# RWKV layer: the triangular inverses of a group's two head pairs, one after the other or in step

## The chip, the cores and the metric

The kernel runs on one core of one Trainium2 chip. The time is what the device takes for one launch, in microseconds (us). Before the change three runs gave 1012.96, 1013.06 and 1014.63 us; the median is 1013.06 us.

## The reference

One layer of a hybrid decoder is applied to 512 prompt tokens and 8 x 8 sample tokens: an RWKV-7 branch and a differential-attention branch on the same normalised input, gates that merge them, an output projection, a squared-ReLU MLP and a final norm. The change concerns the RWKV branch, whose state follows a recurrence over tokens:

```python
def step(S, inp):
    r_t, w_t, k_t, v_t, a_t, b_t = inp
    sa = jnp.einsum('bhij,bhj->bhi', S, a_t)
    S = S * w_t[:, :, None, :] + sa[..., None] * b_t[:, :, None, :] + v_t[..., None] * k_t[:, :, None, :]
    return S, jnp.einsum('bhij,bhj->bhi', S, r_t)
```

There are eight heads of 64. The term `sa` makes each step depend on the step before it. The kernel works on chunks of 64 tokens, in which these dependences form a unit triangular system; its inverse is what the change is about.

## The kernel before

**Work and stages.** The 576 tokens are split into nine chunks of 64 (eight of the prompt, one that holds the sample tokens). Heads are taken in four pairs, `hp` 0 to 3, with two heads on the 128 partitions; pairs 0 and 1 form group 0, pairs 2 and 3 group 1. For each pair a generator `rwkv(hp)` is run from one `yield` to the next. Its first stage makes the decays, the keys and the products of keys within a chunk (`pn`, `pw`, `pa`, `pk`, `pbn`, `pA`), the second transposes values and keys and starts the sample state (`pV`, `pK`, `pI`), the third inverts the triangular matrices, and the later ones finish the sample state and the output. `chain(0)` and `chain(1)` then carry the state through the nine chunks of a group, both pairs together (`pch`, `pY`).

**The inverse.** Each chunk's 64 x 64 matrix is cut into 32 x 32 blocks. A block's inverse grows in four levels, `l` 1 to 4. A level is a series in which every step needs the one before: TensorE multiplies 36 (levels 3 and 4: 32) blocks into `pW`, ScalarE copies `pW` to `W`, TensorE multiplies as many into `pZ`, VectorE adds `pZ` to `X` and transposes `X` into `Y`, and the next level starts from `X`. After the four levels `pWc` and `pC` join the two 32-blocks of a chunk, and ScalarE puts the result and `Y` together in `TT`, which the chain multiplies with. A program's product in plain fp32 shows as two MATMUL records and two LDWEIGHTS records in the trace, so that a visit of 36 blocks is 72 of each; a dense product in fp32r is one of each.

**What lies between.** `take(n)` sends `n` dense products (128 x 128 by 288 or 296 columns) of the weight streams that wait in a list: the projections `ps_z` and the gates `ps_g`. `blocks()` calls `take(9)` behind every visit, so that TensorE has nine dense products while ScalarE or VectorE work on the result of the visit. Behind `pWc` and `pC` there is none. Numbers such as `take(221)` and `take(106)` between the stages set how much dense work lies elsewhere.

**What sets the order.** [...] The framework's scheduler places the instructions by priority, in the order of the program where no priority is given, and lets a later instruction go ahead when an earlier one is not ready by its own estimate; `issue_after` ties dense products behind a given product. All inverses write to one accumulation bank, `tbank`; the chain's `pY` has another, `cbank(1)`.

The last lines of the program's RWKV part, with the stages in the order in which they are called, are in the diff below.

Of the kernel before, what the change touches and what calls it, by code (L numbers as in the profile page):

```python
# [41 lines left out]
def tile_hybrid_step(ctx, tc, xT, xsT, ktab, vtab, s0T, ptab, w_in, vecs, w2a2, g2, lamv,  # L42
# [6 lines left out]
    def pool(name, bufs=1, stack=ctx, **kw):  # L49
        return stack.enter_context(tc.tile_pool(name=name, bufs=bufs, **kw))  # L50
# [4 lines left out]
    ring = {"job": 0}  # L55

    def act(out, in_, func=AF.Copy, **kw):
        ring["act"] = AE.activation(out=out, in_=in_, func=func, **kw)  # L58

    def tt(out, a, b, op, eng=None):  # L60
        ins = (eng or VE).tensor_tensor(out=out, in0=a, in1=b, op=op)  # L61
        if eng is None:
            ring["tt"] = ins
# [7 lines left out]
    def mm(out, lhsT, rhs, start=True, stop=True):  # L71
        ring["mm"] = PE.matmul(out=out, lhsT=lhsT, rhs=rhs, start=start, stop=stop)  # L72
        return ring["mm"]
# [17 lines left out]
    MUL, ADD, SUB, MAX = ALU.mult, ALU.add, ALU.subtract, ALU.max  # L91
# [12 lines left out]
    def tbank(name):  # L104
        return psc.tile([P, 512], F32, tag="t", name=name)

    def cbank(i, name):
        return (psy if i else psc).tile([P, 512], F32, tag=f"c{i}", name=name)
# [107 lines left out]
    def take(n):  # L216

        while waiting and n:
            if next(waiting[0], None) is None:
                waiting.pop(0)  # L220
            else:
                n -= 1
# [41 lines left out]
    gs = pool("gs", 2, stack=ph1)  # L264

    with tc.tile_pool(name="xin", bufs=2, reuse_waits="tile") as xin:
# [6 lines left out]
        for k in range(0, KT, 4):  # L273
            for j in range(3):
                with prio(FEED + 1000 + 10 * k + j):
                    name = f"raw_{'qkv'[j]}0_{k}"
# [142 lines left out]
    def shifted(i):  # L419
        z = zw.tile([P, 1 + NX], F32, tag="z", name=f"Z{i}")  # L420
        GE.memset(z[:, 0:1], 0.0)

        def f(ps, t0, n):
            tt(z[:, 1 + t0:1 + t0 + n], ps, R1[:, t0:t0 + n], MUL)
        yield from stream(w_in[i], KT, xh, xl, HALFX, f, f"z{i}")
        tz = zw.tile([P, 1 + NX], F32, tag="tz", name=f"tz{i}", bufs=1)
        act(tz, z, scale=v(V_MU + i))
        p = zp.tile([P, NT], F32, tag=f"P{i}" if i >= 12 else f"Pt{i // 4}", name=f"P{i}", bufs=1 if i >= 12 else 2)
        m1 = mu1[:, i:i + 1]
        stt(p[:, :NPR], z[:, 1:1 + NPR], m1, tz[:, 0:NPR], MUL, ADD)  # L430
        s3 = lambda a, o: a[:, o:o + NS].rearrange("p (b t) -> p b t", b=NB)
        stt(s3(p, NPR)[:, :, 1:], s3(z, 1 + NPR)[:, :, 1:], m1, s3(tz, 1 + NPR)[:, :, :7], MUL, ADD)
        stt(p[:, NPR::8], z[:, 1 + NPR:1 + NT:8], m1, tz[:, 1 + NT:], MUL, ADD)
        Pt[i] = p

    def zs(hp):
        return [shifted(i) for i in (hp, 4 + hp, 8 + hp)]

    def gate(g):

        gg = gs.tile([P, NT], F32, tag="gg", name=f"gg{g}")

        def ev(ps, t0, n):
            tt(gg[:, t0:t0 + n], ps, R1[:, t0:t0 + n], MUL)
            act(gg[:, t0:t0 + n], gg[:, t0:t0 + n], AF.Tanh, scale=0.5)
        yield from stream(w_in[26 + g], KT, xh, xl, HALF, ev, f"g{g}")
        nc.sync.dma_start(out=gt_d[g], in_=gg)
# [20 lines left out]
    def branch_b(d):  # L468

        if not ob:  # L470
            ob.extend(ob_halves())
        gg = rt.tile([P, NT], F32, tag="T", name=f"gb{d}", bufs=6)
        nc.sync.dma_start(out=gg, in_=gt_d[KT + d])

        def ev(ps, t0, n):
            stt(gg[:, t0:t0 + n], gg[:, t0:t0 + n], 1.0, ps, ADD, MUL)
        yield from stream(w_brb[d], HB, ob[0], ob[1], HALF, ev, f"brb_{d}")
        nc.sync.dma_start(out=gt_d[KT + d], in_=gg)
# [236 lines left out]
    def m3(ap_, n):  # L715
        q, w = ap_.shape
        return ap_.rearrange("p (o w) -> p o w", o=1).broadcast_to([q, n, w])
# [17 lines left out]
    def rwkv(hp):  # L735
        e = hp % 2
# [131 lines left out]
        for g in range(4):  # L868
            gs = slice(32 * g, 32 * g + 32)
            act(DT[gs], ABR[gs, :, 0, 32 * (g % 2):32 * (g % 2) + 32])  # L870
        Y = rt.tile([P, NCH, 32], F32, tag="Y", name=f"Y{hp}", bufs=2)
        X = rt.tile([P, NCH, 32], F32, tag="X", name=f"X{hp}", bufs=2)
# [1 line left out]
        tt(Y, Y, m3(c[:, C_I32:C_I32 + 32], NCH), ADD)  # L874
        VE.transpose(out=X, in_=Y)

        def blocks(ps, lhs, rhs, n):
            for ci in range(n):
                for g in range(4):
                    gs = slice(32 * g, 32 * g + 32)  # L880
                    last = mm(ps[gs, ci * 32:ci * 32 + 32], lhs[gs, ci], rhs[gs, ci])
            with tc.issue_after(last.ins):
                take(9)
            return ps[:, :n * 32].rearrange("p (c s) -> p c s", c=n)

        with tc.issue_after(ring["mm"].ins):
            take(1)
        for l in range(1, 5):

            n = NCH if l < 3 else 8  # L890
            DM = rt.tile([P, NCH, 32], F32, tag="DM", name=f"DM{hp}_{l}")
            tt(DM[:, :n], DT[:, :n], m3(c[:, C_LM + 32 * l:C_LM + 32 * l + 32], n), MUL)
            W = rt.tile([P, NCH, 32], F32, tag="W", name=f"W{hp}_{l}")
            act(W[:, :n], blocks(tbank(f"pW{hp}{l}"), DM, X, n))
            tt(X[:, :n], X[:, :n], blocks(tbank(f"pZ{hp}{l}"), Y, W, n), ADD)
            VE.transpose(out=Y[:, :n], in_=X[:, :n])
        TT = rb_.tile([P, NCH, 64], F32, tag="TT", name=f"TT{hp}")
        pW = tbank(f"pWc{hp}")
        W = rt.tile([P, NCH, 32], F32, tag="W", name=f"Wc{hp}")
        quads = [(slice(64 * par, 64 * par + 32), slice(64 * par + 32, 64 * par + 64)) for par in range(2)]  # L900
        for ci in range(8):
# [1 line left out]
                mm(pW[b1, ci * 32:ci * 32 + 32], ABR[b0, ci, 0, 32:64], X[b0, ci])  # L903
        for b0, b1 in quads:
            act(W[b1, :8], pW[b1, :256].rearrange("p (c s) -> p c s", c=8))
        pC = tbank(f"pC{hp}")
        for ci in range(8):
            for b0, b1 in quads:
                mm(pC[b0, ci * 32:ci * 32 + 32], W[b1, ci], Y[b1, ci])
        for b0, b1 in quads:  # L910
            act(TT[b0, :8, 32:64], pC[b0, :256].rearrange("p (c s) -> p c s", c=8))
            act(TT[b0, :, 0:32], Y[b0])
            act(TT[b1, :, 32:64], Y[b1])
            GE.memset(TT[b0, 8:, 32:64], 0.0)
            GE.memset(TT[b1, :, 0:32], 0.0)

        own[e] = ST, KBt, TT, ABR, pc
        yield
# [113 lines left out]


    gens = [rwkv(hp) for hp in range(4)]

    def run(*stages):
        for hp in stages:
            while Pt[8 + hp] is None:
                take(2)
            next(gens[hp], None)  # L1040

    waiting += zs(1) + zs(2) + zs(3) + [gate(g) for g in range(KT, 2 * KT)]
    ga = [gate(g) for g in range(KT)]
    waiting += ga[:5]
    run(0, 0)
    take(221)
    run(0, 1, 1)
    take(106)
    run(1)
    chain(0)  # L1050
    run(2, 0, 1, 2, 3)
    take(291)
    run(2, 0, 1, 3)
    take(38)
    run(3)
    waiting += [x for d in range(KT) for x in [branch_b(d)] + ga[5:][d:d + 1]]
    run(0, 1)
    chain(1)
# [237 lines left out]
    for t0, n in LAST:  # L1296
        span, last = slice(t0, t0 + n), []
# [172 lines left out]
```

## Time and profile before

| | |
|---|---|
| median of three runs | 1013.06 us |
| the profiled execution's own time | 1013.38 us |
| its span, first to last instruction | 1011.6 us |
| TensorE, matmul records (PE) | 977.1 us busy, 10012 records |
| TensorE, weight loads (PEld) | 917.7 us busy, 10012 records |
| VectorE (DVE) / ScalarE (ACT) / GpSimd (POOL) | 694.2 / 496.2 / 101.3 us busy |
| mean granted clock of TensorE | 0.994 |
| the four inverses | at 225 to 247, 281 to 302, 394 to 414 and 425 to 446 us |

A busy TensorE is not a TensorE at its peak: matmuls overlap and their ends are modelled, so that the distance from start to start says what one costs. In the rows of the trace `[0.87 <-issue]` is idle time of that engine just before the row, and what ended it; "issue" stands for a start that no semaphore of the profile explains. Runs of equal instructions are merged into one row with a count, and the time in the second column reaches from the start of the first to the end of the last.

### The profile page before, as it was taken

What the parts mean: (1) busy time and instruction counts of PE and PEld (TensorE: products, weight loads), DVE (VectorE), ACT (ScalarE), POOL (GpSimd) and SP (SyncE); (2) the same over time, 40 slices, a digit from 0 to 9 for tenths busy, and PEclk for the clock granted to TensorE, in tenths of its full rate; (3) what the DMA queues carried; (4) which work ended last, traced back from release to release, by engine and by line L of the source; (5) the groups of instructions that cost most, each with busy time, mean ns of one, the idle gap of its engine ahead of it and who ended that gap; (6) DMA issues with size and microseconds to landing.
All of it is one profiled execution on the core that took longest, in us unless ns stands there. A gap on an engine that the chain in (4) does not pass through costs nothing. (4 is left out here: it accounts for less than half of the span.)

```text
span 1011.6 us, 24409 instructions
## 1 busy us (share of the span) xinstructions
PE 977.1 (97%) x10012; PEld 917.7 (91%) x10012; DVE 694.2 (69%) x1445; ACT 496.2 (49%) x1086; POOL 101.3 (10%) x179
## 2 busy tenths in 40 slices
PE   9999999999999999999989999999999999999996
PEld 8999889898888788878889999999999999999996
DVE  6697565964965788345579888966666666666644
ACT  7575563454453353453244666644444444444732
POOL 2511104001010421000210111000000000000001
PEclk9999999999999999999999999999999999999998
DMA  7312663121111235222367633232222222221402
GB/s 272 132 65 97 208 214 100 52 65 44 53 47 56 68 109 172 79 71 89 114 205 222 197 122 99 75 103 85 94 84 87 92 85 84 85 84 43 132 6 94
DMA packets 50833, 105.75 MB, mean 105 GB/s; under 512 B 6066, under 2 KB 8114, under 8 KB 50594
## 3 DMA queue, kind: packets, MB, share of 16 engines
q1 hardware_dynamic: 47442, 96.95, 29.8%
q0 software_dynamic: 1648, 5.35, 1.4%
q10 hardware_dynamic: 1632, 1.89, 0.5%
q8 instruction: 79, 1.29, 0.5%
q14 instruction: 32, 0.26, 0.1%
HBM read 89.38 MB, written 14.78 MB: 103 GB/s over the span
## 5 line engine op out<-in xcount | busy, mean ns | idle before, releaser
L72 PE MATMUL ps_dn<-q,hi_dn 128*128 128x288 f32 x768 | 154.8, 296 | 0.0
L72 PEld LDWEIGHTS ps_dn<-q,hi_dn 128*128 128x128 f32 x768 | 122.9, 188 | 1.4
L72 PE MATMUL ps_dn<-q,lo_dn 128*128 128x288 f32 x384 | 113.3, 295 | 0.0
L72 PE MATMUL ps_g<-xh,hi_g 128*128 128x288 f32 x256 | 80.3, 314 | 0.0
L72 PE MATMUL ps_g<-xh,lo_g 128*128 128x288 f32 x256 | 79.2, 309 | 0.6 <-issue 0.6
L72 PE MATMUL ps_g<-xl,hi_g 128*128 128x288 f32 x256 | 79.3, 310 | 0.0
L72 PEld LDWEIGHTS ps_dn<-q,lo_dn 128*128 128x128 f32 x384 | 72.2, 188 | 0.0
L72 PE MATMUL ps_z<-xh,hi_z 128*128 128x296 f32 (+1 forms) x224 | 67.7, 302 | 1.2 <-DVE Z L61 0.7
L72 PE MATMUL ps_z<-xl,hi_z 128*128 128x288 f32 (+1 forms) x224 | 68.2, 305 | 0.3 <-issue 0.3
L72 PE MATMUL ps_z<-xh,lo_z 128*128 128x288 f32 (+1 forms) x224 | 68.4, 305 | 0.0
L61 DVE TENSOR_TENSOR ya<-ya,ps_dn 128x288 f32<-128x288 f32 x96 | 43.4, 452 | 29.4 <-PE ps_dn L72 29.4
L58 ACT ACTIVATE hi_dn<-raw_dn 128x512 fp32r<-128x512 f32 x48 | 30.1, 628 | 56.1 <-PE ps_dn L72 56.1
L1206 PE MATMUL ua<-h_b,hi 128*128 128x288 f32 x256 | 53.3, 299 | 0.9 <-ACT p L58 0.9
L1206 PE MATMUL ux<-h_t,hi 128*128 128x288 f32 x256 | 52.3, 296 | 0.0
L72 PEld LDWEIGHTS ps_g<-xh,hi_g 128*128 128x128 f32 x256 | 49.0, 192 | 3.2 <-issue 1.6
L58 ACT ACTIVATE c<-c 128x288 f32<-128x288 f32 x112 | 48.5, 440 | 6.6 <-DVE c L61 4.9
L72 PEld LDWEIGHTS ps_g<-xl,hi_g 128*128 128x128 f32 x256 | 49.0, 191 | 2.5 <-issue 0.8
L72 PEld LDWEIGHTS ps_g<-xh,lo_g 128*128 128x128 f32 x256 | 48.9, 191 | 1.4
L58 ACT ACTIVATE hi<-a 128x1024 fp32r<-128x1024 f32 (+1 forms) x32 | 27.0, 845 | 43.1 <-PE ps_dn L72 34.9
L61 DVE TENSOR_TENSOR lo<-s,hi 128x1024 fp32r<-128x1024 f32 x32 | 39.2, 1224 | 10.5 <-ACT hi L58 10.4
L72 PE MATMUL ps_dn<-q,w 128*128 128x320 f32 (+1 forms) x336 | 46.3, 298 | 0.0
L72 PEld LDWEIGHTS ps_dn<-q,w 128*128 128x128 f32 x336 | 45.3, 190 | 0.1
(399 smaller groups left out, 2813.8 us busy)
## 6 DMA issues: line engine op xcount, KB each, us to landing
a<-in_w_up_dram SPq DMA_DIRECT2D x32, 512.0 KB, 3.3
raw_dn<-in_w_down_dram SPq DMA_DIRECT2D x64, 256.0 KB, 2.8
raw_g<-in_w_in_dram SPq DMA_DIRECT2D x32, 256.0 KB, 3.1
raw_z<-in_w_in_dram SPq DMA_DIRECT2D x28, 256.0 KB, 2.8
gt_d<-gg SPq DMA_DIRECT2D x16, 288.0 KB, 2.3
g<-gt_d SPq DMA_DIRECT2D x16, 288.0 KB, 3.4
kp<-in_ktab_dram SPq DMA_DIRECT2D x16, 256.0 KB, 5.0
vp<-in_vtab_dram SPq DMA_DIRECT2D x16, 256.0 KB, 4.2
```

What stands on the lines that cost most here:

```text
L58: ring["act"] = AE.activation(out=out, in_=in_, func=func, **kw)
L61: ins = (eng or VE).tensor_tensor(out=out, in0=a, in1=b, op=op)
L72: ring["mm"] = PE.matmul(out=out, lhsT=lhsT, rhs=rhs, start=start, stop=stop)
L1206: ring["mm"] = PE.matmul(out=ps[:, :288], lhsT=l[:, k], rhs=hb[blk][:, h, k], start=start and i == 0, stop=i == 11, skip_group_check=skip)
```

## The change

A visit now yields, and a new function `invert` drives two generators in turn: one visit of the first pair, one of the second, then twelve dense products. The second pair of a group writes to the chain's bank `cbank(1)`, which is free then. `take(9)` in `blocks` is gone, and twelve dense products now also stand behind the double visits of `pWc` and of `pC`. The stages of the second pair that come ahead of its inverse are called earlier, and the counts of the dense work between the stages are set anew (221, 106 and 291, 38 become 221, 120 and 320, 38).

```diff
-        def blocks(ps, lhs, rhs, n):
+        def blocks(name, lhs, rhs, n):
+            ps = cbank(1, name) if e else tbank(name)
             for ci in range(n):
                 for g in range(4):
                     gs = slice(32 * g, 32 * g + 32)
-                    last = mm(ps[gs, ci * 32:ci * 32 + 32], lhs[gs, ci], rhs[gs, ci])
-            with tc.issue_after(last.ins):
-                take(9)
+                    mm(ps[gs, ci * 32:ci * 32 + 32], lhs[gs, ci], rhs[gs, ci])
             return ps[:, :n * 32].rearrange("p (c s) -> p c s", c=n)
 
-        with tc.issue_after(ring["mm"].ins):
-            take(1)
         for l in range(1, 5):
...
-            act(W[:, :n], blocks(tbank(f"pW{hp}{l}"), DM, X, n))
-            tt(X[:, :n], X[:, :n], blocks(tbank(f"pZ{hp}{l}"), Y, W, n), ADD)
+            act(W[:, :n], blocks(f"pW{hp}{l}", DM, X, n))
+            yield True
+            tt(X[:, :n], X[:, :n], blocks(f"pZ{hp}{l}", Y, W, n), ADD)
             VE.transpose(out=Y[:, :n], in_=X[:, :n])
+            yield True
...
-        pW = tbank(f"pWc{hp}")
+        pW = cbank(1, f"pWc{hp}") if e else tbank(f"pWc{hp}")
...
+        yield True
-        pC = tbank(f"pC{hp}")
+        pC = cbank(1, f"pC{hp}") if e else tbank(f"pC{hp}")
...
+    def invert(*hps):
+
+        with tc.issue_after(ring["mm"].ins):
+            take(1)
+        more = True
+        while more:
+            for hp in hps:
+                more = next(gens[hp], None)
+            with tc.issue_after(ring["mm"].ins):
+                take(12)
+
...
     run(0, 0)
     take(221)
-    run(0, 1, 1)
-    take(106)
-    run(1)
+    run(1, 1)
+    take(120)
+    invert(0, 1)
     chain(0)
     run(2, 0, 1, 2, 3)
-    take(291)
-    run(2, 0, 1, 3)
+    take(320)
+    run(0, 1, 3)
     take(38)
-    run(3)
+    invert(2, 3)
```

The order on TensorE at level 3 of group 0, before (`pW` and `pZ` are the visits of pair 0 alone, `ps_z` the dense products, of which nine stand between two visits):

```order
L72 MATMUL pZ_3414<-W_2_3365,Y_3259 32x32 x36
L72 MATMUL ps_z_1_3249<-xh,lo_z_0_3241 128x296
...
L72 MATMUL pW_3465<-X_3260,DM_3_3462 32x32 x32
L72 MATMUL ps_z_1_3249<-xh,lo_z_1_3245 128x296
...
L72 MATMUL pZ_3531<-W_3_3464,Y_3259 32x32 x32
```

The same place in the changed program (`pZ_4135` and `pW_4222` are of pair 0, `pZ_4170` and `pW_4259` of pair 1; `ps_g` are the dense products, twelve between two double visits):

```order
L72 MATMUL pZ_4135<-W_3_4051,Y_3643 32x32 x32
L72 MATMUL pZ_4170<-W_3_4088,Y_3694 32x32 x32
L72 MATMUL ps_g_0_4042<-xh,lo_g_1_4039 128x288
...
L72 MATMUL pW_4222<-X_3644,DM_4_4219 32x32 x32
L72 MATMUL pW_4259<-X_3695,DM_4_4256 32x32 x32
L72 MATMUL ps_g_1_4043<-xh,lo_g_0_4035 128x288
...
L72 MATMUL pZ_4305<-W_4_4221,Y_3643 32x32 x32
L72 MATMUL pZ_4340<-W_4_4258,Y_3694 32x32 x32
```

Two visits of different pairs now stand back to back. In group 1 all ten visits are double; in group 0 the first `pW` and `pZ` of the two pairs still stand apart, and the other eight are double. So there are 12 + 10 = 22 stretches of small products where there were 40.

The end of group 0's inverses on ScalarE, before (`TT` with the number 4490 is that of pair 1, which the chain waits for):

```order
L58 ACTIVATE TT_4490<-Y_4086 32x9x32 x2
L58 ACTIVATE Wc_4492<-pWc_4491 32x256 x2
L58 ACTIVATE TT_4490<-Y_4086 32x9x32
L58 ACTIVATE hi_g_0_5218<-raw_g_0_5214 128x512
L58 ACTIVATE gg_4287<-gg_4287 128x288
L58 ACTIVATE TT_4490<-pC_4511 32x8x32 x2
L58 ACTIVATE TT_4490<-Y_4086 32x9x32
```

The same place in the changed program (`TT_4405` is pair 0's, `TT_4426` pair 1's):

```order
L58 ACTIVATE Wc_4407<-pWc_4406 32x256 x2
L58 ACTIVATE Wc_4428<-pWc_4427 32x256 x2
L58 ACTIVATE TT_4405<-pC_4459 32x8x32 x2
L58 ACTIVATE TT_4426<-Y_3694 32x9x32
L58 ACTIVATE TT_4426<-pC_4486 32x8x32
L58 ACTIVATE TT_4426<-Y_3694 32x9x32
L58 ACTIVATE TT_4426<-pC_4486 32x8x32
L58 ACTIVATE TT_4426<-Y_3694 32x9x32 x2
```

All four copies of `Y` into pair 1's `TT` now stand behind the copies out of pair 0's `pC`; before, three of pair 1's four went ahead of its own `pC`.

## The prediction

> **What bounds the kernel now.** I read the page's busy times, then the timeline of the four inverses on TensorE and its weight loads, then who waits for what, then the DMA queues.
>
> ```profile
> span 1011.6 us, 24409 instructions
> PE 977.1 (97%) x10012; PEld 917.7 (91%) x10012; DVE 694.2 (69%) x1445; ACT 496.2 (49%) x1086; POOL 101.3 (10%) x179
> q8 instruction: 79, 1.29, 0.5%
> ```
>
> TensorE sets the time. As the dense products are only shifted, the change can move the end only through what lies between TensorE's instructions: switches between small and dense products, and waits. The third row matters later: 79 packets of 16 KB; TensorE's 2 x 10012 records at 256 per packet make 78.
>
> Two visits of pair 0 and the dense products between them:
>
> ```profile
> 225.54 0.82 PE L72 MATMUL pW<-X,DM 32*32 32x32 f32 x72
> 226.29 0.40 PE L72 MATMUL ps_z<-xh,lo_z 128*128 128x288 f32 x1
> 226.52 0.29 PE L72 MATMUL ps_z<-xh,hi_z 128*128 128x288 f32 x1
> ...
> 227.45 0.29 PE L72 MATMUL ps_z<-xl,hi_z 128*128 128x288 f32 x1
> 227.68 0.82 PE L72 MATMUL pZ<-W,Y 32*32 32x32 f32 x72
> 228.42 0.40 PE L72 MATMUL ps_z<-xh,lo_z 128*128 128x288 f32 x1
> L72 PE MATMUL pW<-X,DM x1088: 185/192/213, 225.5 to 439.9; 32*32 32x32 f32 x182
> ```
>
> From 226.52 to 227.45 seven dense products start: 0.133 us each. The first and the last of the nine hold 0.23 us, 0.10 more each. The 72 small ones start over 0.82 less one duration of 0.19, that is 0.63 us (9 ns each), but the first dense product comes 0.75 us after the first small one: the last small one holds 0.12, or 0.11 more. So an alternation costs 0.10 + 0.10 + 0.11 = 0.31 us. The nine fully cover ScalarE's copy here.
>
> Now the weight loads in pair 2's inverse:
>
> ```profile
> 397.43 0.29 PEld L72 LDWEIGHTS pW<-X,DM 32*32 32x32 f32 x25 [0.87 <-issue]
> ...
> 399.15 0.71 PEld L72 LDWEIGHTS pZ<-W,Y 32*32 32x32 f32 x72 [0.16 <-issue]
> ...
> 401.29 0.20 PEld L72 LDWEIGHTS pW<-X,DM 32*32 32x32 f32 x12 [0.16 <-issue]
> 402.41 0.54 PEld L72 LDWEIGHTS pW<-X,DM 32*32 32x32 f32 x52 [0.91 <-issue]
> ...
> 404.38 0.64 PEld L72 LDWEIGHTS pZ<-W,Y 32*32 32x32 f32 x64 [0.16 <-issue]
> ...
> 406.25 0.19 PEld L72 LDWEIGHTS ps_g<-xh,hi_g 128*128 128x128 f32 x1 [0.75 <-issue]
> ```
>
> TensorE stops in the middle of a visit, twelve products into a `pW` whose operands are all there, and no semaphore explains it. Between the second and the third stop lie 52 + 9 + 64 + 3 = 128 weight loads (nine and three of them dense), with their matmuls 256 instructions; between the first two 25 + 9 + 72 + 9 + 12 = 127. That is one packet of q8 each. I read the stops as TensorE waiting for its next block of 256 instructions. Between two stops one block passes: 4.98 and 3.84 us. The others:
>
> ```profile
> 235.65 0.19 PEld L72 LDWEIGHTS ps_z<-xl,hi_z 128*128 128x128 f32 x1 [0.52 <-issue]
> 293.73 0.20 PEld L72 LDWEIGHTS pZ<-W,Y 32*32 32x32 f32 x13 [0.62 <-issue]
> 410.08 0.22 PEld L72 LDWEIGHTS pZ<-W,Y 32*32 32x32 f32 x16 [0.23 <-issue]
> 430.14 0.39 PEld L72 LDWEIGHTS pW<-X,DM 32*32 32x32 f32 x34 [0.22 <-issue]
> 437.80 0.15 PEld L72 LDWEIGHTS pZ<-W,Y 32*32 32x32 f32 x6 [1.03 <-issue]
> ```
>
> From 406.25 to 410.08 is again a block: 3.83 us. All eight stops together are 5.2 us. Elsewhere a block lasts long:
>
> ```profile
> q8 instruction: 21, 0.34, 0.4%
> ```
>
> This is the DMA view from 600 to 950 us, where only large products run: a block every 16.7 us. There a fetch of under 4 us is never seen. In the inverses 72 + 9 products are 162 instructions in 2.14 us (225.54 to 227.68), so 256 in 3.4 us: just faster than a block is fetched.
>
> **The change part by part.**
>
> *Switches.* 40 stretches of small products become 22: 18 x 0.31 = 5.6 us less.
>
> *Instructions per time.* The small products themselves stay. A double visit of levels 1 and 2 with its twelve dense products holds 2 x (144 + 12) = 312 instructions. Free of waits it takes 0.63 + 0.01 + 0.75 = 1.39 us for the small ones and 227.68 - 226.29 = 1.39 plus 3 x 0.133, or 1.79, for the dense ones: 3.18 us, so 256 instructions in 2.61 us. At levels 3 and 4 the 128 small ones are 16 x 0.009 = 0.14 us shorter (1.25 us), and 280 instructions take 3.04 us, 256 in 2.77. The mean is 2.69 us per block, against the 3.83 us or more that a block took between stops. So nearly every block now ends in a stop.
>
> Eight double visits of a group hold 4 x 312 + 4 x 280 = 2368 instructions, 9.25 blocks. The block that follows the one in use has been loaded in the slow stretch ahead, which takes one off: 8 blocks a group, 16 in all. The last two double visits (2 x (64 + 12) = 152 instructions in some 2.9 us) are slow enough.
>
> The price of a block is the unknown. From below 3.4 us, the pace at which the program before ran between stops: 16 x (3.4 - 2.69) = 11.4 us. From above the mean of the three periods, (4.98 + 3.84 + 3.83) / 3 = 4.22: 24.5 us. The 4.98 came while much else was being loaded, and twelve dense products per 3.75 us need fewer weights than nine per 2.14. I take 3.75, just under the two that agree: 16 x 1.06 = 17.0 us.
>
> [...]
>
> *Stops that go.* The eight of before are in the new count, so 5.2 us come off.
>
> *Waits for data.* A `pZ` visit is followed by VectorE's work for both pairs:
>
> ```profile
> 227.39 0.42 DVE L61 TENSOR_TENSOR DM<-DT,cst_sb 128x256 f32<-128x256 f32 x1
> 228.54 0.46 DVE L61 TENSOR_TENSOR X<-X,pZ 128x288 f32<-128x288 f32 x1 [0.73 <-PE pZ L72]
> 229.03 0.48 DVE L896 STREAM_TRANSPOSE Y<-X 128x288 f32<-128x288 f32 x1
> 290.51 0.75 PE L72 MATMUL pW<-X,DM 32*32 32x32 f32 x64 [0.47 <-DVE X L61]
> ```
>
> A level of two pairs needs 2 x (0.42 + 0.46 + 0.48) = 2.7 us of VectorE, and two rounds last 6.2 us even without stops. The next `pW` of pair 1 needs both `X` and, in this order, pair 0's transpose: 0.46 + 0.48 + 0.46 = 1.4 us, of which the first 0.46 can run under pair 1's small products, against 1.79 us of dense cover. I count no change, with 0.5 us either way for the wait at 290.51. `cbank(1)` adds none: the bank's next write needs the copy of its last contents as data anyway.
>
> *The end of a group.* The chain's second product needs both pairs' `TT`:
>
> ```profile
> 301.19 0.44 ACT L58 ACTIVATE TT<-Y 32x288 f32<-32x288 f32 x1
> 302.64 0.77 ACT L58 ACTIVATE TT<-pC 32x256 f32<-32x256 f32 x2
> 303.16 0.30 PE L72 MATMUL pch<-R,TT 64*64 64x64 f32 x2 [0.21 <-ACT TT L58]
> ```
>
> In the new order ScalarE has four copies of `pC` and four of `Y` behind the first `pC`: 2 x 0.77 + 4 x 0.44 = 3.3 us. TensorE has pair 1's `pC` (about 0.6 us) and twelve dense products (1.8) to cover it, and waits some 0.9 us before `chain(0)`, where it waited 0.21: 0.7 us more. Queued behind it are the first steps of the chain. In group 1 other products stand between, so nothing there.
>
> *The dense counts.* Before, 221 + 106 + 291 + 38 and 4 x 73 in the inverses: 948. Now 221 + 120 + 320 + 38 and 2 x 121: 941. Seven products (0.9 us) run later instead; they cost the same there.
>
> Sum: -5.6 + 17.0 - 5.2 + 0.7 = +6.9 us. The profiled execution took 1013.38 us around its span of 1011.6, 0.3 us above the median of 1013.06. So 1020.2, rounded to **1020 us**.
>
> **The rivals.**
>
> *Fetching does not bind (faster).* If blocks come sooner, since less else is loaded, or if the stops have another cause that does not scale with the pace, the double visits run at 3.1 us each. With the stops as before the sum is -5.6 + 0.7 = -4.9: 1008 us. It decides at the price of a block: the sum is zero where 16 x (p - 2.69) = 5.6 + 5.2 - 0.7, at p = 3.32 us. For it: between 225.54 and 230 us no stop shows. Against it: blocks at 3.83 and 3.84 us right after a stop, where nothing but the fetch could be late. [...]
>
> *Data come too late.* If blocks come in time but VectorE, between dense work of its own as at 290.51, makes TensorE wait 0.47 us at each of the 16 double visits of the four levels, 7.5 us come back: -5.6 - 5.2 + 7.5 + 0.7 = -2.6, 1011 us. Against it are the 2.7 us of work in 6.2.
>
> *The clock.* Busy time and granted clock in three stretches:
>
> ```profile
> 399.50:402.90 3.40, 2.60 (x127) 2.29 (x113) 1.91 (x4) 0.44 (x1) 0.00 (x0) 1.00 0.62 196
> 415.60:419.00 3.40, 2.39 (x42) 1.95 (x41) 0.00 (x0) 2.77 (x10) 0.00 (x0) 1.00 0.14 48
> 419.00:422.40 3.40, 3.40 (x16) 3.40 (x16) 0.46 (x1) 1.57 (x6) 0.00 (x0) 0.51 0.00 0
> ```
>
> After a stretch with TensorE busy for 2.39 of 3.40 us the clock fell to half for 3.4 us; after one with 2.60 it did not. The new rounds, busy for 2.69 of 3.75 us (2.44 of 3.40), lie between. A fall costs half of 3.4, 1.7 us; with four in each group 1020 becomes 1034 us.
>
> **How the numbers follow.** The forecast gets 0.70, the fetch that does not bind 0.15, late data 0.10, the clock 0.05. The likeliest case alone runs from 11.4 to 24.5 us for the blocks, so from +1.3 to +14.4: 1014.5 to 1028. The range reaches down to take in the case of late data and leave out most of the faster one: 1009 to 1027. About 2 us (0.2%) is what a measurement of this kernel can tell from no change. Faster: 0.15 and a third of the late data, 0.18. The same: the rest of the late data and the lowest edge of the forecast, 0.10. Slower: 0.72.
>
> **What would show it.** Right: in the changed kernel's inverses TensorE's weight loads stop for about 1 us every 256 instructions, mostly inside the small products, with "issue" as the releaser; two double visits take near 7.3 us instead of 6.2; q8's packets come every 3.5 to 4 us there; the waits of loads for `pW` and `pZ` on "issue" more than double. Wrong: double rounds of 3.2 us without stops (the first rival), waits on VectorE's `X` (the second), a granted clock under 1.00 in the inverses (the third), or a wait at the start of `chain(0)` well above 1 us, which I sized from the order alone.

## The result, and the profile after

In seven runs of each on one chip the changed kernel takes 1019.85 us (median; 1016.30 to 1021.73) and the kernel before 1013.04 (1009.45 to 1014.63). The ratio is 1.0065, with a 95% interval of 1.0045 to 1.0084: slower by 6.8 us. The prediction was 1020 us. The profiled execution of the changed kernel took 1019.11 us around a span of 1017.3, 5.7 us more than that of the kernel before (1013.38 around 1011.6).

The page of the changed kernel, span and busy times:

```profile
span 1017.3 us, 24397 instructions
PE 973.8 (96%) x10012; PEld 918.5 (90%) x10012; DVE 696.2 (68%) x1445; ACT 496.8 (49%) x1086; POOL 100.6 (10%) x179
```

TensorE has the same 10012 matmuls and is busy for 3.3 us less than before, in a span that is 5.7 us longer. So it stands still for longer. Where it does so is seen in the timeline of its weight loads, the view in which the prediction read the stops. First the double visits of group 0, of which only the rows with a stop are shown, and ahead of them one visit that stands in a single row (the number in brackets is idle time just before the row):

```profile
268.15 1.54 PEld L72 LDWEIGHTS pW<-X,DM 32*32 32x32 f32 x144 [0.17 <-DVE Z L61]
...
272.28 1.18 PEld L72 LDWEIGHTS pZ<-W,Y 32*32 32x32 f32 x117 [0.40 <-issue]
277.47 0.19 PEld L72 LDWEIGHTS ps_g<-xh,hi_g 128*128 128x128 f32 x1 [2.60 <-issue]
280.93 0.17 PEld L72 LDWEIGHTS pW<-X,DM 32*32 32x32 f32 x2 [1.19 <-issue]
288.78 0.32 PEld L72 LDWEIGHTS pW<-X,DM 32*32 32x32 f32 x26 [0.27 <-issue]
292.35 0.43 PEld L72 LDWEIGHTS pZ<-W,Y 32*32 32x32 f32 x39 [0.53 <-issue]
```

Then those of group 1:

```profile
407.46 1.33 PEld L72 LDWEIGHTS pW<-X,DM 32*32 32x32 f32 x144 [0.16 <-issue]
410.62 0.68 PEld L72 LDWEIGHTS pZ<-W,Y 32*32 32x32 f32 x69 [0.16 <-issue]
413.20 0.76 PEld L72 LDWEIGHTS pZ<-W,Y 32*32 32x32 f32 x75 [1.91 <-issue]
421.21 1.23 PEld L72 LDWEIGHTS pZ<-W,Y 32*32 32x32 f32 x128 [0.62 <-issue]
425.04 0.18 PEld L72 LDWEIGHTS pZ<-W,Y 32*32 32x32 f32 x3 [2.61 <-issue]
433.99 0.33 PEld L72 LDWEIGHTS pZ<-W,Y 32*32 32x32 f32 x28 [0.39 <-issue]
437.44 0.44 PEld L72 LDWEIGHTS pW<-X,DM 32*32 32x32 f32 x40 [0.46 <-issue]
441.29 0.54 PEld L72 LDWEIGHTS pZ<-W,Y 32*32 32x32 f32 x52 [0.77 <-issue]
445.40 0.19 PEld L72 LDWEIGHTS ps_g<-xl,hi_g 128*128 128x128 f32 x1 [0.66 <-issue]
```

These rows show twelve stops, with idle times of 0.40 + 2.60 + 1.19 + 0.27 + 0.53 = 5.0 us in group 0 and 7.4 us in group 1, 12.4 us in all; the eight of before made 5.2. They lie within a visit (after 69 of 144 loads, after 126 of 128) or among the dense products, and no semaphore ends them. Where nothing stops, the round is as fast as it should be: 407.46 to 410.62, 3.16 us.

What does end them is a packet on q8, the queue of instructions. The packets' own times are in the traces: the one ahead of the stop that ends at 277.47 ran from 275.13 to 276.08 us, the one ahead of 280.93 from 278.51 to 279.51. All twelve stops end 1.2 to 1.6 us after the end of such a packet, and so do the eight of before (1.3 to 1.5 us). Other waits that the rows put down to "issue" do not: the two 0.81-us waits of `ps_g` behind `pF` (355.88 and 510.88 us) come over 10 us after the last packet.

The three rows of waits on "issue" for the tiles of the inverses, before:

```profile
PEld pZ L72 <- issue: 4.3, 18, 1.0
PEld pW L72 <- issue: 4.2, 15, 0.9
PEld ps_g L72 <- issue: 2.4, 3, 0.8
```

and after (us in total, times, the longest):

```profile
PEld pZ L72 <- issue: 8.7, 14, 2.6
PEld ps_g L72 <- issue: 4.9, 4, 2.6
PEld pW L72 <- issue: 3.1, 9, 1.2
```

They come less often, since there are fewer switches (each has its 0.16 us in these rows), and last longer: 16.7 us in place of 10.9.

**Where the 5.7 us come from.** For each pair of neighbouring matmuls I took the median distance from start to start that such a pair has in the trace of before, and summed it over the order of each program. What a start comes later than that was put down to a stop on "issue" in the inverses, to half clock, to a wait for data of over 0.15 us (from 200 to 560 us), or to the rest. From the first to the last matmul's start, in us:

| | order without waits | stops | half clock | waits for data | rest | sum |
|---|---|---|---|---|---|---|
| before | 961.2 | 6.0 | 3.1 | 11.3 | 22.3 | 1003.9 |
| changed | 956.5 | 13.3 | 6.1 | 13.8 | 19.9 | 1009.6 |
| difference | -4.7 | +7.3 | +3.0 | +2.5 | -2.4 | +5.7 |

The stops are 0.8 to 0.9 us larger here than in the rows of weight loads, since this counts what the matmuls lose. "Rest" holds many small deviations and isn't explained further. The first column is an estimate that hangs on which pairs are held to be alike: told apart by the shapes of the products alone, the order of the change comes out 3.7 us shorter than before in place of 4.7, and the difference moves into the rest.

The clock is not a peculiarity of these two executions. Over its seven runs the changed kernel was granted 0.989 of the full clock on average, the kernel before 0.993 to 0.994 in its 71 runs beside the experiments below. If TensorE is busy throughout, 0.004 of 1015 us is some 4 us (an estimate), so that about half of the 6.8 us that the change costs goes by way of the clock.

### The profile page after: what moved, and what is told of

The parts are those of the page before. It is cut to its first block, busy times and chain, and to the rows that moved or that the text cites. A ratio compares the mean times of both kernels' runs of the same rounds, so it can differ in the third digit from the quotient of the medians.

```text
span 1017.3 us, 24397 instructions
## 1 busy us (share of the span) xinstructions
PE 973.8 (96%) x10012; PEld 918.5 (90%) x10012; DVE 696.2 (68%) x1445; ACT 496.8 (49%) x1086; POOL 100.6 (10%) x179
```

## Experiments on the cause: instructions per time, or something else

The theory: TensorE stops because 256 instructions are used up sooner than the next 256 are there; the doubled visits with twelve dense products are only a denser stream. The rival: the stops come with the inverses as such (their operands, their banks, the doubling), and would stay at any pace. The expectations below reckon with 3.3 to 3.8 us or more for a block; the shortest between two stops in any of these traces is 3.45 us. The later times are all against the kernel before on the same chip, which took 1012.79 us in the first set of runs, 1013.48 in the second and 1012.31 in the third.

**Fewer instructions for the same small products.** The tiles of the four levels in bf16, in both kernels:

```diff
-        Y = rt.tile([P, NCH, 32], F32, tag="Y", name=f"Y{hp}", bufs=2)
+        Y = rt.tile([P, NCH, 32], BF16, tag="Yb", name=f"Y{hp}", bufs=2)
...
-            DM = rt.tile([P, NCH, 32], F32, tag="DM", name=f"DM{hp}_{l}")
+            DM = rt.tile([P, NCH, 32], BF16, tag="DM", name=f"DM{hp}_{l}")
```

and DT, X and W alike, with fp32 results at the last level. The changed kernel:

> The changed kernel with the tiles of the inverse's four levels (DT, DM, X, Y, W) in bf16; only the last level's results are written in fp32. The inverse is then computed with fewer digits than the reference asks for. A small product is one matmul and one weight load instead of two of each, so a double round of 2 x (72 + 12) = 168 instructions takes about 3.18 - 0.63 = 2.55 us, 256 instructions 3.9 us: slower than the 3.3 to 3.8 us that a block took between stops. Theory (the pace of instructions is what cost): the small products lose half of 32 visits x 0.63 us = 10 us, and the 13.1 us of stops go too, so 1020 - 10 - 13 = 997 us, range 992 to 1003; 994 if the three half-clock windows behind the stops go with them. Rival (the stops belong to the doubled visits or to their operands, not to the count of instructions): 1020 - 10 = 1010 us with stops left. Second rival: the rounds become so short that VectorE's X and Y come late; then waits of PEld on DVE X of several us.

The kernel before:

> The kernel before with the same tiles in bf16 (the same loss of digits). Theory: small products -10 us, its eight stops (5.2 to 6 us) gone: 1013 - 10 - 6 = 997 us, range 993 to 1002. Beside the changed kernel with bf16 tiles the sign of the whole change should turn round: with no stops in either, the change keeps only its 4.7 us of saved switches, less about 1 us at the start of chain(0) and up to 2.5 us of longer data waits, so the changed one should be 0 to 5 us faster (bf16 against bf16), where in fp32 it was 6.8 us slower. Rival (stops not from the count of instructions): the changed one stays some 6 us slower in bf16 too.

Measured: the changed kernel 991.38 us (987.99 to 993.53), ratio 0.9776 (0.9750 to 0.9802); the kernel before 999.60 us (999.07 to 1001.15), ratio 0.9854 (0.9825 to 0.9884). One round of the changed one at level 3 and the start of the next:

```profile
405.42 0.56 PEld L73 LDWEIGHTS <-Y 32*32 32x32 bf16 x64 [0.17 <-issue]
407.82 0.55 PEld L73 LDWEIGHTS <-DM 32*32 32x32 bf16 x64 [0.17 <-DVE Y L901]
```

The round lasts 2.40 us and holds 2 x (64 + 12) = 152 instructions, 256 in 4.0 us, and no visit is broken: what is left of idle time ahead of a visit in both groups is the 0.16 to 0.17 us of a switch, at two of them 0.2 us more; the granted clock is 0.99 on average from 215 to 450 us. Same doubling, same banks, same twelve dense products, no stops. So the rival falls as far as doubling and banks go; the operands did change their type here, and for them the burst below decides. And the sign of the change turns round: 8.2 us faster in bf16, where it was 6.8 us slower in fp32. I had expected 0 to 5. Part of the surplus is that the kernel before, whose visits are now 1.7 us apart, waits for data inside its inverses. The weight loads, and the matmuls that start with them:

```profile
391.65 0.31 PEld L73 LDWEIGHTS <-DM 32*32 32x32 bf16 x35 [0.35 <-issue]
396.11 0.26 PEld L73 LDWEIGHTS <-DM 32*32 32x32 bf16 x31 [0.79 <-issue]
...
391.64 0.41 PE L73 MATMUL pW<-X,DM 32*32 32x32 bf16 x36 [0.36 <-DVE X L62]
396.11 0.37 PE L73 MATMUL pW<-X,DM 32*32 32x32 bf16 x32 [0.81 <-DVE X L62]
```

Both stand one load into a `pW` visit. Between them lie 35 + 9 + 36 + 9 + 1 + 1 = 91 loads (one of them of `pV`) in 4.46 us, less than the 128 of a block, so they are not stops of the kind above. The rows of the matmuls name what TensorE waited for: VectorE's `X`. By the same account as in the table (medians here over these two traces) the changed kernel saves 7.4 us of order, 2.4 of waits and 2.0 of half clock.

**A burst far from the inverses.** The kernel before with small products that depend on nothing, among the large products of the MLP:

```diff
+            if i == 0 and ch in (3, 5):
...
+                    for j in range(640):
+                        gq = slice(32 * (j % 4), 32 * (j % 4) + 32)
+                        cq = 32 * (j // 4 % 16)
+                        mm(pbu[gq, cq:cq + 32], onesP[gq, :32], onesP[gq, :32])
```

> The kernel before, with two bursts added in the MLP, far from the inverses: 640 fp32 products of 32x32 each on a constant tile, with no operand to wait for, no wait on another engine and a result that nothing reads; 2560 instructions, ten blocks of 256 each. At the second burst, eight extra loads of 256 KB that nothing reads go through another queue. Theory (a block can't be had faster than every 3.3 to 4.2 us): each burst lasts nine or ten times that, 30 to 40 us, with a stop every 256 instructions, and the kernel 1013 + 60 to 80 = 1073 to 1093 us; the second burst, with the extra loads, is the longer one. Rival (instructions are fetched ahead and cost nothing; stops in the inverses have another cause): 1280 matmul records x 9 ns = 11.5 us for each burst, 1013 + 23 = 1036 us.

Measured: 1113.38 us, ratio 1.097 (1.093 to 1.101), 100 us more, where theory said 60 to 80 and the rival 23. The weight loads of the first burst:

```profile
763.64 2.54 PEld L72 LDWEIGHTS pbu<-onesP 32*32 32x32 f32 x184 [0.25 <-issue]
768.18 1.17 PEld L72 LDWEIGHTS pbu<-onesP 32*32 32x32 f32 x128 [1.99 <-issue]
771.92 1.80 PEld L72 LDWEIGHTS pbu<-onesP 32*32 32x32 f32 x128 [2.57 <-issue]
...
797.86 0.41 PEld L72 LDWEIGHTS pbu<-onesP 32*32 32x32 f32 x24 [2.22 <-issue]
```

Exactly 128 loads, with their matmuls 256 instructions, and then a stop, again and again. From 768.18 to 797.86 pass eight blocks: 3.71 us each, at full clock (1.00 in the stretch of the first 128 loads, which take 1.17 us) as at half (0.50 from 770.2 us on, 1.80). All nine stops end 1.3 to 1.5 us after a packet on q8. The operands are constant and the result is read by nobody, so only the instructions can be late. This is the price that the prediction set at 3.75. The fetch is not hidden here: 256 instructions go out in 1.2 to 1.8 us, the first stop comes after 184 loads in a row, and the next ones after each 256 instructions.

The part that I had missed is a lesson on switches. The scheduler set the first 24 small products of the burst one by one between dense ones:

```profile
746.65 0.24 PE L72 MATMUL pbu<-onesP 32*32 32x32 f32 x2
746.83 0.40 PE L72 MATMUL ps_dn<-q,hi_dn 128*128 128x288 f32 x1
747.15 0.24 PE L72 MATMUL pbu<-onesP 32*32 32x32 f32 x2
```

One small and one dense product take 0.50 us; without the switch they would take 0.133 + 2 x 0.009 = 0.15, so an alternation costs 0.35 us (the prediction had 0.31). From 749.8 us on it cost more, at half clock (0.50; 0.78 us a pair), so that 24 pairs filled the 17.0 us from 746.65 to 763.64, 13 us more than their work. With the nine blocks of the burst, 33 us, that is most of its 50. The extra loads of the second burst settle nothing, since they had landed before it: its blocks between two stops last 3.47 to 4.02 us, as in the first (3.47 to 4.01).

**Fourteen dense products in the kernel before**, still one visit after another, to slow the stream without doubling anything:

```diff
             with tc.issue_after(last.ins):
-                take(9)
+                take(14)
...
-    take(221)
+    take(181)
...
-    take(106)
+    take(66)
...
-    take(291)
+    take(213)
```

> The kernel before with fourteen dense products behind each single visit in place of nine; the dense counts between the stages are cut by as many (181, 66, 213, 36), so that 948 dense products lie ahead of the second chain as before. Nothing is in step. A visit with its fourteen products is 172 instructions in about 2.8 us, 256 in 4.2 us. Theory (TensorE's instructions come in blocks of 256, each taking 3.3 us or more): no stop with 'issue' as releaser is left in the inverses, where the kernel before had eight of 5.2 us idle together; the clock falls less; about 1006 us (1004 to 1009). Rival (the stops come with the number of small products, or with the bank or the data they wait for, not with the pace of instructions): the same products and the same number of stops, 1011 to 1014 us.

Measured: 1018.45 us (1016.03 to 1018.96), ratio 1.0047 (1.0027 to 1.0067). The stops went, as said: 0.2 us are left of 6.0. But the kernel became slower, not faster. Three rows of its waits, of weight loads in the stages between the inverses; before, that of `pbn` was 1.3 us and the two of `pA` did not occur:

```profile
PEld pbn L72 <- DVE rkp L66: 2.5, 2, 1.2
PEld pA L72 <- POOL TT L915: 2.3, 1, 2.3
PEld pA L72 <- DVE KB L61: 1.6, 1, 1.6
```

The waits for data rose from 11.3 to 22.2 us. The 160 dense products that went into the inverses (40, 40, 78 and 2 fewer between the stages) were the cover of the stages between them. That is where the gain that I expected went: dense products are the scarce thing here, and an inverse pays for slack with a stage's.

**Six dense products behind each single visit, in step.** The order of the pairs as in the change, but no doubling:

```diff
             for hp in hps:
                 more = next(gens[hp], None)
-            with tc.issue_after(ring["mm"].ins):
-                take(12)
+                with tc.issue_after(ring["mm"].ins):
+                    take(6)
```

> The changed kernel, in step, but with six dense products behind each single visit in place of twelve behind two: the same dense work, no double visit, as many switches as before. A visit with its six is 156 instructions in about 1.75 us, 256 in 2.85 us. Theory: nearly as many stops as in the change and none of the gain from fewer switches, so 1018 to 1024 us, at or above the changed kernel. Rival (it is the double visit as such that costs, by its length or by the work that it puts on VectorE and ScalarE at once): with single visits as before, the time is back at 1011 to 1014 us.

Measured: 1017.29 us (1015.41 to 1018.95), ratio 1.0045 (1.0032 to 1.0058). Slower than before without a single double visit, so the rival falls; the time is just under the 1018 to 1024 of the theory, and a little below that of the change. Some of its stops in group 0:

```profile
275.23 0.54 PEld L72 LDWEIGHTS pW<-X,DM 32*32 32x32 f32 x52 [1.15 <-issue]
278.96 0.64 PEld L72 LDWEIGHTS pZ<-W,Y 32*32 32x32 f32 x64 [0.64 <-issue]
282.53 0.14 PEld L72 LDWEIGHTS pZ<-W,Y 32*32 32x32 f32 x6 [1.31 <-issue]
```

They stand 3.73 and 3.57 us apart, a block each. It has 9.7 us of stops by the account, between the 6.0 of nine dense products a visit and the 13.3 of twelve for two. The order without waits is 961.4 us, as before: no switch is saved, and none was expected to be.

## Experiments on the balance: how many dense products

If the pace is the cause, more dense products behind a double visit must take the stops away while the gain from fewer switches is left; if the cover of the stages is scarce, it must stop paying somewhere. The edit is one number in `invert` and, against it, those between the stages, here for twenty:

```diff
             with tc.issue_after(ring["mm"].ins):
-                take(12)
+                take(20)
...
-    take(221)
+    take(181)
     run(1, 1)
-    take(120)
+    take(80)
...
-    take(320)
+    take(240)
```

The edit does one thing more than its number says. In these versions, with less dense work between the stages, the first visits of a group's first pair start early, among the products of the stages: level 1 is no longer visited in step in either group, and is in part broken into pieces. The versions have 24 (eighteen), 30 (twenty), 27 (twenty-two) and 26 (twenty-four) stretches of small products in their traces, where the change has 22 and the kernel before 40.

Eighteen, with 191, 90 and 260:

> The changed kernel with 18 dense products behind a double visit instead of 12 (and 191, 90, 260, 38 between the stages). 256 instructions then take about 2.69 x (3.15 + 0.8) / 3.15 x 294 / 306 = 3.2 us, just under the 3.3 to 3.8 us of a block, so a few short stops stay (some 5 us), and ten dense products a stage more are left as cover than with 20. Theory: between 1008 and 1012 us, level with or a little above the 1009.5 of 20 products. If the cover of the stages were what decides, below 1008; if the stops, above 1012.

Twenty:

> The changed kernel with twenty dense products behind each double visit in place of twelve; the counts between the stages are cut by as many (181, 80, 240), 941 in all as in the change. A double visit is 328 instructions in about 4.2 us, 256 in 3.3 us, the pace of the kernel before. Theory: the stops shrink to a few of some tenths of a us, the clock stays up, and the gain from fewer switches is left: about 1004 us (1001 to 1008). Rival (double visits make TensorE wait for data, or the second bank costs): the stops stay, and 1017 to 1021 us.

Twenty once more, in another set of runs:

> The version with 20 dense products behind a double visit (181, 80, 240, 38 between the stages) once more, beside its neighbour with 22. Theory (a double round of 20 dense products lasts 4.1 us, 256 instructions 3.6 us, so few blocks are late, and the cover left between the stages still holds): again 1008 to 1011 us, faster than the kernel before by 2 to 5 us. Rival (the first result belongs to how the blocks happened to fall in those executions): 1012 to 1017, as with 18.

Twenty-two, with 171, 70 and 220:

> The changed kernel with 22 dense products behind a double visit and 171, 70, 220, 38 between the stages. Theory: stops as few as with 20 (4 to 5 us in all), and 20 products less between the stages than with 20, half-way to the 24 whose uncovered stages cost some 6 us: 1010 to 1014 us. If the cover gives way abruptly, 1015 as with 24; if it is the stops alone, 1008 or less.

Twenty-four, with 161, 60 and 200:

> The changed kernel with twenty-four dense products behind each double visit; counts between the stages 161, 60, 200, again 941 in all. A double visit is 336 instructions in about 4.8 us, 256 in 3.6 us. Theory: hardly a stop is left; about 1003 us (1000 to 1008), unless the stages between the inverses lack dense work (120 is now 60) and wait for VectorE instead, which would show as waits at pn, pk, pA and give back some us. Rival as for twenty: 1017 to 1021 us.

Measured, with the account of each profiled execution as above (order without waits, stops, half clock, waits for data, in us):

| dense products | median, us | ratio to before | 95% interval | order | stops | half clock | data |
|---|---|---|---|---|---|---|---|
| 12 (the change) | 1019.85 | 1.0065 | 1.0045 to 1.0084 | 956.5 | 13.3 | 6.1 | 13.8 |
| 18 | 1017.08 | 1.0024 | 1.0006 to 1.0043 | 956.2 | 8.2 | 8.5 | 13.9 |
| 20 | 1009.47 | 0.9969 | 0.9953 to 0.9984 | 954.2 | 4.4 | 3.9 | 13.0 |
| 20 again | 1009.59 | 0.9963 | 0.9944 to 0.9982 | 954.2 | 5.1 | 9.3 | 12.0 |
| 22 | 1011.77 | 0.9994 | 0.9978 to 1.0010 | 953.4 | 3.9 | 12.3 | 16.9 |
| 24 | 1015.45 | 1.0025 | 1.0002 to 1.0048 | 953.3 | 5.6 | 9.5 | 18.7 |

The order column is the estimate named above, and it fits badly with the stretches just counted: by shapes alone the order of these versions is 907.2 to 909.5 us, that of the change 906.3 and that of before 910.0. So how much of the saved switches they keep is not shown.

The version with twenty is faster than both kernels, by 0.3% against the one before, in both sets. Its rounds at levels 3 and 4 in group 0, three without a stop, and the longest stop that is left in group 1:

```profile
268.68 1.20 PEld L72 LDWEIGHTS pW<-X,DM 32*32 32x32 f32 x128 [0.16 <-DVE Z L61]
272.77 1.20 PEld L72 LDWEIGHTS pZ<-W,Y 32*32 32x32 f32 x128 [0.17 <-issue]
276.93 1.20 PEld L72 LDWEIGHTS pW<-X,DM 32*32 32x32 f32 x128 [0.17 <-issue]
...
421.21 0.14 PEld L72 LDWEIGHTS pZ<-W,Y 32*32 32x32 f32 x3 [1.67 <-issue]
```

A round of 2 x (128 + 20) = 296 instructions lasts 4.1 us, 256 in 3.6, about what a block takes. With twenty-four the rounds are slower still, yet stops of up to 1.68 us are left. The mean pace of a round does not decide alone: in the burst one block was there in time and each of the next nine came late (a stop after every 128 loads), as if no more than one were loaded ahead; so each block counts by what it holds. The long stops that are left stand behind blocks that fall on one double visit. In the traces the block ahead of the stop of 2.27 us with eighteen (425.74 to 429.58) holds 126 small loads and 1 dense one, that ahead of the 1.67 us with twenty (417.76 to 421.21) 125 and 3, that ahead of the 1.68 us with twenty-four (426.80 to 430.53) 123 and 5. Without the stop such a block lasts 1.6 to 2.1 us, whatever the rounds around it take.

With twenty-four the waits of the stages go up by 5.7 us against twenty, as the row of the uncovered `pA` shows that twenty does not have:

```profile
PEld pA L72 <- DVE KB L61: 1.4, 2, 1.2
```

I had expected 1003 for it and 1004 for twenty; the waits between the stages and the half clock were not in those sums. Eighteen missed its 1008 to 1012 as well: its stops are 8.2 us, not 5, and its half clock is the 8.5 us of five stretches. Twenty-two was expected at 1010 to 1014 and came there. That 18 and 20 are 7.6 us apart is more than the stops alone explain (8.2 against 4.4 us). Half clock differs between executions of one and the same kernel (below), but the granted clock of every run is on record: 0.9885 on average with eighteen, 0.9906 and 0.9902 in the two sets with twenty. The difference of 0.002 over some 1010 us is about 2 us (an estimate), and on the chip of eighteen the kernel before took 0.7 us more than on that of twenty. Together with the 3.8 us of stops that is most of the 7.6.

## Why the prediction was right, point by point

**Stops (predicted 17.0 us new, 5.2 old ones gone, so +11.8; measured 12.4 against 5.2 in the rows of weight loads, +7.2).** The mechanism is as predicted, and the mean price of a stop too: 12.4 / 12 = 1.03 us against 1.06, from stops of 0.27 to 2.61 us. A block between two stops took 3.46 us (277.47 to 280.93), 3.57, 3.83, 3.45, 3.85 and 4.11 us, a mean of 3.71 where I had taken 3.75, and once 5.19. The term was mis-sized by the number of stops, 16 against 12, in three ways. I counted eight double level visits in each group, though in group 0 the first `pW` and `pZ` of the two pairs stand apart, which leaves six: two blocks less. I let the round of `pWc` go as slow enough, and a block ended in it (445.40): one more. And three of the 15 block ends that remain show no stop: between 280.93 and 288.78, 413.20 and 421.21, and 425.04 and 433.99 lie two blocks each. In each of these stretches TensorE ran at half clock for a while (granted clock 0.50, a dense product every 0.24 us where it was 0.13), which made the rounds slow enough for the fetch. So two terms that I had held apart, stops and clock, eat each other's time.

**Switches (predicted -5.6).** The rows bear the size out: two visits of pair 0 with nine dense products each took 2 x 2.14 us, a double one with twelve takes 3.16, and six dense products more would be 0.80, so a double visit saves 0.32 us, 18 of them 5.8 (an estimate). In the account the order without waits became 4.7 us shorter (3.7 by shapes alone); the rest fell by 2.4, part of which may be the same. The burst put the price of one at 0.35 us against 0.31. A round without a stop was to last 3.18 us and lasts 3.16.

**Waits for data (predicted none, 0.5 us either way).** In the double visits themselves this held: the `pW` at 268.15 starts 0.17 us after the load before it, a switch and no wait on `X`. The 2.5 us more in the account lie elsewhere: some 0.45 of them at `chain(0)` (next point), the rest in the stages between, whose places shifted.

**The start of `chain(0)` (predicted a wait of 0.9 us, +0.7).**

```profile
301.79 0.30 PE L72 MATMUL pch<-R,TT 64*64 64x64 f32 x2 [0.66 <-ACT TT L58]
```

In its idle time before this product TensorE waited 0.66 us for `TT`, where it was 0.21: 0.45 us more. The wait was rightly placed from the order alone, and sized a little too long.

**The clock (a rival with 0.05, in the sum with nothing).** This is the step that failed, though it moved the time less than the rival had it. The 3.40 us ahead of each of the three falls in the changed kernel's inverses (matmuls busy in the first column behind the length, the granted clock third from the end):

```profile
274.50:277.90 3.40, 1.03 (x7) 0.68 (x5) 2.48 (x6) 1.42 (x2) 0.00 (x0) 0.99 0.17 63
...
411.00:414.40 3.40, 1.61 (x126) 1.45 (x115) 0.88 (x3) 0.00 (x0) 0.00 (x0) 1.00 0.09 25
...
421.20:424.60 3.40, 1.34 (x127) 1.23 (x128) 0.93 (x2) 0.00 (x0) 0.00 (x0) 1.00 0.32 81
```

I had weighed the mean round, busy for 2.44 of 3.40 us, against the 2.39 after which the clock fell before. But stops are not spread evenly: three of them last 1.91 to 2.61 us, and the 3.40 us around such a stop are busy for 1.0 to 1.6 us only. The stop of 2.61 us shows why a mean misleads: the block ahead of it, 421.21 to 425.04, holds 128 small loads and no dense product, 1.23 us of work, while the two blocks on either side of it hold 24 dense products. The stretches at half clock that follow, of 6.8, 3.4 and 6.8 us, make 17 us where there were 6.8, and cost 3.0 us more.

The 2.39 was no threshold either. The kernel before had another fall, at 364.4 us, and the stretch ahead of it was busy throughout:

```profile
361.00:364.40 3.40, 3.40 (x51) 3.10 (x50) 2.36 (x7) 1.50 (x6) 0.27 (x1) 1.00 0.67 227
```

So the share of busy time does not tell by itself when the clock falls; what does was not found.

So the forecast of 1020 came out with errors that cancel: 4.6 us too much for stops, against 3.0 for the clock and 2.5 for other waits that it did not have. The sign and the cause were foreseen; that the number came out to the microsecond was luck. (The sum itself has a slip without weight: 1013.38 + 6.9 is 1020.3, not 1020.2.) Of the signs that it named, three held (stops every 256 instructions, packets of q8 8 in 32 us, the wait at `chain(0)`). Two did not: two rounds together lasted 9.0 us in group 1, not 7.3 (eight from 407.46 to 443.66, four pairs in 36.2 us), because fewer but longer stops met half clock; and the waits of `pW` and `pZ` on "issue" went from 8.5 to 11.8 us and not to the double, since I forgot that these rows count the 0.16 us of each switch. Less those, they went from 3.2 (33 times) to 8.1 us (23 times).

The rival in which the fetch does not bind is ruled out by the burst and by the bf16 pair. The late data were not seen in the double visits.

## What to carry to other kernels

Count the instructions, not only the work: here 256 of them on TensorE took about 3.7 us to come (3.45 to 4.11 in most blocks between two stops), and where 256 were used in clearly less TensorE stopped, on the operands of the inverses as on the constant ones of the burst. The count is to be made block by block: with twenty dense products, 3.6 us per 256 on the mean, TensorE still stopped for 1.67 us behind a block of 125 small loads and 3 dense ones. Packing small matmuls closer saves switches (0.3 us each) only as long as it does not bring such blocks; twenty dense products a double visit were worth it, twelve were not, and with half the instructions twelve were. And dense work that covers a wait is a budget: what is moved into one stage is missed in another.

## What the runs showed of the hardware that was not expected

**The fetch is slow on its own.** I had thought that other transfers slow it. In the burst the blocks took 3.5 to 4.0 us while the data queues were nearly still; from 764 to 798 us they moved one load of 0.26 MB, at the start:

```profile
q1 hardware_dynamic: 144, 0.26, 2.7%
q8 instruction: 9, 0.15, 1.9%
```

Whether traffic adds to it was not settled: the blocks of the changed kernel (between two block ends) in which the DMA engines were busy for 0.02 to 0.16 of the time lasted 3.45 to 3.85 us, those with 0.22 to 0.42 lasted 3.83 to 5.19. In the longest block of the changed kernel, 5.19 us (272.28 to 277.47), and in one of 4.92 us that ends at 413.20, the packet on q8 began 2.85 and 2.75 us after the start of the block, where it was 1.0 to 1.9 behind the other stops; what held it back was not shown.

**A block ahead, not more.** Stops came one block apart, with the next block late again. In the burst the first 184 loads ran through, 2.54 us, and the first stop, of 1.99 us, stood behind them. With 128 loads to a block, the block before had ended after the first 56 of them, without a stop; its successor was there, and the one after that was not. In the changed kernel the packet of the next block began 1.02 to 2.85 us after each of the twelve stops had ended, so after TensorE had gone over to a new block: of the 3.46 us from 277.47 to 280.93, 1.04 passed until the packet began, 1.00 was the packet, and 1.42 passed until TensorE went on. The transfer is less than a third of the price. So in these runs TensorE behaves as if it held the block in use and one more.

**Half clock differs between executions of one kernel.** The traces show stretches of 3.4 us (from 364.4 and from 419.0 us in the kernel before), of 6.8 (from 277.9 us in the changed one) and of 13.7 (below), multiples of 3.4. The same kernel with twenty dense products, profiled twice, had full clock in one execution and 13.7 us of half clock in the other at the same place of the program (390 to 405 us):

```profile
390.00:405.00 15.00, 13.15 (x312) 11.31 (x312) 12.33 (x27) 9.21 (x26) 3.33 (x6) 1.00 0.37 117
```

```profile
390.00:405.70 15.70, 13.67 (x210) 11.03 (x211) 9.26 (x21) 9.06 (x26) 1.80 (x1) 0.57 0.25 78
```

Their spans are 1005.3 and 1010.7 us. The account puts 5.4 us between their half clocks. What made the difference was not shown. So the clock is what a single trace of these kernels can't be trusted for, and the spread of the times (1004.5 to 1012.6 in that set) is of this size.

**A busy TensorE can fall to half clock.** In the burst, at its first alternations with dense products:

```profile
746.40:749.80 3.40, 3.40 (x23) 2.13 (x21) 2.93 (x5) 3.27 (x9) 0.00 (x0) 0.99 0.18 70
749.80:753.20 3.40, 3.40 (x15) 2.10 (x13) 0.00 (x0) 0.06 (x1) 0.00 (x0) 0.50 0.28 77
```

The first stretch shows matmuls busy for all of its 3.40 us and the clock still falls behind it. What the profile calls busy there is mostly the 0.35 us of each switch, and the weight loads were busy for 2.13 us. But they are no better sign: ahead of the fall at 364.4 us in the kernel before, shown above, the loads were busy for 3.10 of 3.40 us.
